# First attention input of a decoder trunk: 32-token blocks of x turned on VectorE, features in the order 512h+4p+k

## The chip, the cores and the metric

The kernel runs on one core of a Trainium2 chip. The metric is the device time of one execution in microseconds; three executions of the kernel before gave a median of 1459.0 us (1458.99 to 1459.35). The input is one sequence of 512 tokens with 1024 features in float32.

TensorE (PE) multiplies; its weight loads are told apart as PEld. VectorE (DVE) and ScalarE (ACT) work on tiles elementwise, GpSimd (POOL) builds small tables and issues some transfers, and SyncE (SP) issues most loads. Each engine executes its instructions in the order in which the program gives them, and semaphores hold an instruction until what it needs is there.

## The reference, cut to what matters

```python
def rms_norm(x, g):
    y = x * lax.rsqrt(jnp.mean(x * x, axis=-1, keepdims=True) + RMS_EPS)
    return y * g

for layer in range(2):
    h = rms_norm(x, norm_mix_pre[layer])
    if layer % 2 == 0:
        h = dilated_attention_mixer(h, attn_w_qkv[j], attn_w_o[j], rel_bias)   # begins with h @ w_qkv
    else:
        h = rglru_mixer(h, ...)                                               # begins with h @ w_in
    x = x + rms_norm(h, norm_mix_post[layer])
    h = rms_norm(x, norm_ffn_pre[layer])
    h = conv_ffn(h, ...)
    x = x + rms_norm(h, norm_ffn_post[layer])
```

The change concerns the very first product, `rms_norm(x, norm_mix_pre[0]) @ w_qkv`. The product sums over the 1024 features, so any order of the features gives the same result as long as x, the norm weights and the rows of `w_qkv` use the same one.

## The kernel before, in words

**Numbers in two parts.** Every float32 operand of a large product is split into a rounded part `hi` (made by ACT) and the rest `lo` (made by DVE), and each product of 128 features is three matmuls: hi x hi, lo x hi, hi x lo.

**Features on the partitions.** TensorE sums over partitions, so x must stand with features on the 128 partitions: `hT` is a pair (hi, lo) of tiles with eight groups of 128 features by 512 tokens. The input x arrives with tokens on the partitions. It is loaded as eight half tiles (`x_half(t, i)`: 128 tokens t, 512 features i), and `first_transposed(t, i)` (L338) turns a half tile by four TensorE transposes of 128 by 128 into one PSUM bank; ACT writes hi from it (L345) and DVE writes lo (L346).

**The norm.** The norm weights multiply the rows of the first weights when those are split (`split_normed`, L139; `whi` on ACT in L143, `wlo` on DVE in L144). The factor of each token, one over the root of its mean square, is applied to the results instead of to x. `first_squares(i)` (L348) sums the squares of four half tiles on ACT, and `first_roots` (L355) makes the factors `first_y`. POOL writes them to memory as a row (`yrow`, L367) and loads the row onto all partitions (`roots`, L368), because queries and keys stand with tokens along the free axis.

**The order of the work.** The order on each engine is the order in which the program is written. Weights come in chunks of 1 MB through three buffers `raw`; `pump` splits them a piece ahead of use into eight pairs of buffers, and `load` issues the next chunk on SP's queue once a buffer is free. The attention begins with `first_values` (L654): the values of the first heads, four token tiles by four weight pieces, each `product(t, u)` six matmuls (L664) of 128 by 512. Between the products stand the eight `first_transposed`, the squares, and the splitting of the weights; the four results are scaled by `first_y` in the end (L707). Then `feat_tiles` makes queries and keys for two heads as four units of 24 matmuls (L255), and `qk` (L649, L651) multiplies each by the `roots` row on DVE. One unit later `local` issues the scores S (L773) of the first head, which need its query and its key.

**The start of the loads.** At the end of the kernel function the first loads are written out by hand: the norm weights as eight rows of 128 (turned by TensorE at L1077 and copied at L1079), then half tiles of x and pieces of the first two weight chunks (`w_part`) in turns, all on SP's queue. A few matmuls on ones (`warm`) come ahead.

Of the kernel before, what the change touches and what calls it, by code (L numbers as in the profile page):

```python
# [18 lines left out]
P = 128  # L19
# [55 lines left out]
def kernel(  # L75
# [42 lines left out]
    def gen(dt=F32, s="g"):  # L118
        return gp.tile([P, 512], dt, tag="g", name=nm(s))

    def psum(s="ps"):
        return pp.tile([P, 512], F32, tag="ps", name=nm(s))
# [86 lines left out]
    def take(i, j):  # L209
        while (i, j) not in units:  # L210
            before = state["live"]
            pump(1)
            assert before != state["live"]
        return units[i, j]

    def done(n=1):
        state["live"] -= n
# [17 lines left out]
            tick()  # L235

    def w_cols(w, c0, normed=False):
        plan.append(("feat", KD, 256, [(w[:, c0 : c0 + 256].rearrange("(k p) c -> p k c", p=P), KD)], 0 if normed else None))

    def w_value(w, *cuts):  # L240

        for i in range(2):
            rows = w[i * 512 : (i + 1) * 512, :]
            plan.append(
                ("value", 4, 512, [(rows[:, c0 : c0 + n].rearrange("(k p) c -> p k c", p=P), n) for c0, n in cuts], 4 * i)
            )

    def w_rows(w, r0):
# [89 lines left out]
    def first_transposed(t, i):  # L338

        ps = psum("tr")  # L340
        for k in range(4 * i, 4 * i + 4):
            nc.tensor.transpose(ps[:, k % 4 * P : (k % 4 + 1) * P], x_sb[:, t, k * P : (k + 1) * P], ident)
        ps3 = ps.rearrange("p (k c) -> p k c", k=4)
        hi, lo = (h[:, 4 * i : 4 * i + 4, t * P : (t + 1) * P] for h in first_hT)
        nc.scalar.activation(hi, ps3, AF.Copy)  # L345
        nc.vector.tensor_tensor(lo, ps3, hi.bitcast(F32), op=ALU.subtract)  # L346

    def first_squares(i):  # L348
        for t in range(4):
            junk = gen(s="junk")  # L350
            nc.scalar.activation(
                junk, x_sb[:, t, i * 512 : i * 512 + 512], AF.Square, accum_out=first_ss[i][:, t : t + 1]
            )
# [249 lines left out]
    def attention(hT, post, pre):  # L603
# [50 lines left out]
        def first_values(vs):  # L654

            ids = [chunk(), chunk()]
            banks = [psum("v") for _ in range(4)]

            def product(t, u, which=range(6)):
                W = take(ids[u // 2], u % 2)  # L660
                steps = [(k, a, b) for a, b in PASSES for k in (2 * u, 2 * u + 1)]
                for n in which:
                    k, a, b = steps[n]
                    mm(  # L664
                        banks[t],
                        hT[a][:, k, t * P : (t + 1) * P],
                        W[b][:, k % 2, :],
                        start=u == n == 0,
                        stop=u == 3 and n == 5,
                    )  # L670

            first_transposed(0, 0)
            warm(WARM - 2)
            product(0, 0, range(4))
            first_transposed(1, 0)
            product(0, 0, range(4, 6))
            product(1, 0)
            product(0, 1, range(3))
            first_transposed(2, 0)
            product(0, 1, range(3, 6))  # L680
            product(1, 1)
            first_transposed(3, 0)
            product(2, 0)
            first_squares(0)
            product(2, 1)
            first_transposed(0, 1)
            product(3, 0)
            take(ids[1], 0)
            first_transposed(1, 1)
            product(3, 1)  # L690
            done(2)
            first_transposed(2, 1)
            product(0, 2)
            take(ids[1], 1)
            first_transposed(3, 1)
            for t in (1, 2, 3):
                product(t, 2)
            first_squares(1)
            y = first_roots()
            first_y.append(y)  # L700
            for t in range(4):
                product(t, 3)
                pump(1)
            done(2)
            for t in range(4):
                o = gen(s="v")
                nc.scalar.activation(o, banks[t], AF.Copy, scale=y[:, t : t + 1])  # L707
                vs.append(o)
# [341 lines left out]
    def w_part(i, k0, k1):  # L1050
        nc.sync.dma_start(raws[i][:, k0:k1, :], plan[i][3][0][0][:, k0:k1, :])

    st = gen(s="st")
    nc.scalar.dma_start(st[:KD, :P], norm_mix_pre[0].rearrange("(k p) -> k p", p=P))
    for i in range(2):
        raws[i] = wp.tile([P, 4, 512], F32, tag="raw", name=nm("raw"), bufs=RAW_BUFS)
    state["dma"] = 2
# [2 lines left out]
    w_part(0, 1, 2)  # L1060
    x_half(1, 0)
    w_part(0, 2, 4)
    x_half(2, 0)
    x_half(3, 0)
    w_part(1, 0, 2)
    x_half(0, 1)
    x_half(1, 1)
    w_part(1, 2, 4)
    x_half(2, 1)
    x_half(3, 1)  # L1070
    one.append(gen(F32R, "one"))
    nc.vector.memset(one[0].bitcast(F32), 1.0)
    warm_ps = psum("warm")
    warm(WARM)
    root_table()
    cols_ps = psum("cols")
    nc.tensor.transpose(cols_ps[:, :KD], st[:KD, :P], ident[:KD, :KD])  # L1077
    first_w.append(cp.tile([P, KD], F32, tag="first_w", name="first_w"))
    nc.vector.tensor_copy(first_w[0], cols_ps[:, :KD])  # L1079
    hT = attention(hT, (norm_mix_post, 0), (norm_ffn_pre, 0))  # L1080
    hT = ffn(0, hT, (norm_ffn_post, 0), (norm_mix_pre, 1))
    hT = lru(hT, (norm_mix_post, 1), (norm_ffn_pre, 1))
# [29 lines left out]
```

## Time and profile before

| | |
|---|---|
| median of three runs | 1459.0 us |
| profiled execution | 1459.46 us |
| its span (first to last instruction) | 1457.7 us |
| PE busy | 1448.4 us (99%) |
| VectorE busy | 862.4 us (59%) |
| ScalarE busy | 669.5 us (46%) |
| GpSimd busy | 134.4 us (9%) |
| moved by DMA | 172.24 MB, 118 GB/s in the mean |

The profile is of one execution. A row of the timeline gives the start in us from the start of the span, the length in us, the engine, the line, the instruction and its operands as out<-in; in square brackets stand the idle time of the engine just before it and who ended that. SPq is SP's queue of issued loads. A row of the groups gives the line, engine, operation and shape with its count, then busy us in total, the mean ns of one, and the idle time before them. The chain of waits follows the work that ended last back through what released it.

### The profile page before, as it was taken

The page shows a single profiled execution, that of the slowest core. Times are in us where ns is not written, and L with a number is a line of the kernel's source. Part 1 is how long each engine was busy: PE and PEld are TensorE (multiplying, and loading weights), DVE is VectorE, ACT ScalarE, POOL GpSimd, SP SyncE. Part 2 cuts the span into 40 slices and gives each one's busy share as a digit, 9 for nine tenths or more (in the row PEclk, how much of TensorE's full clock was granted, in tenths as well). Part 3 has the DMA queues.
Part 4 walks back from the last instruction along what each step waited for, and adds up shares of the span by engine and source line. Part 5 has one row for each costly group of instructions (what it writes and reads, how often), then busy time and mean ns, then how long its engine had stood idle before and what let it go on. Part 6 is the DMA issues. An engine that isn't in the chain of part 4 may idle for free.

```text
span 1457.7 us, 18749 instructions
## 1 busy us (share of the span) xinstructions
PE 1448.4 (99%) x6894; PEld 1217.2 (84%) x6894; DVE 862.4 (59%) x1916; ACT 669.5 (46%) x1516; POOL 134.4 (9%) x275
## 2 busy tenths in 40 slices
PE   9999999999999999999999999999999999999998
PEld 7888888888888898888888888888898888888886
DVE  5656636464646875555654338769776555564333
ACT  6645526262615553443343235589453433444321
POOL 0450513040402100000000001000100000000000
PEclk9999999999999999999999999999999999999999
DMA  6653536364636342322323222432433223223201
GB/s 205 211 151 98 170 117 194 116 180 135 194 120 210 95 137 88 116 87 87 116 87 116 98 90 87 130 116 73 130 102 116 87 94 109 87 98 131 89 1 58
DMA packets 123572, 172.24 MB, mean 118 GB/s; under 512 B 7960, under 2 KB 100600, under 8 KB 123480
## 3 DMA queue, kind: packets, MB, share of 16 engines
q1 hardware_dynamic: 112744, 144.95, 30.7%
q0 software_dynamic: 10144, 25.04, 6.2%
q8 instruction: 54, 0.88, 0.3%
q10 hardware_dynamic: 592, 1.05, 0.2%
q14 instruction: 38, 0.31, 0.1%
HBM read 155.72 MB, written 15.29 MB: 117 GB/s over the span
## 4 chain that ended last, share of the span: by engine, by line
PE 92%; ACT 4%; DVE 3%; issue 1%; DMA 0%; POOL 0%; DVEq 0%; ACTq 0%
PE ps L255 54%; PE acc L255 24%; PE v L723 7%; PE v L664 1%; DVE xb L924 1%; PE S L811 1%; PE O L797 1%; PE O L866 1%; PE S L773 1%; DVE wlo L150 1%; ACT sig L945 1%; ACT whi L149 1%; PE tr L331 1%; DMA ft<-turned 0%; ACT sig L964 0%
## 5 line engine op out<-in xcount | busy, mean ns | idle before, releaser
L255 PE MATMUL ps<-hT,whi 128*128 128x512 f32 (+1 forms) x2752 | 801.4, 375 | 0.0
L255 PEld LDWEIGHTS ps<-hT,whi 128*128 128x128 f32 x2752 | 503.7, 188 | 91.5
L255 PE MATMUL ps<-hT,wlo 128*128 128x512 f32 (+1 forms) x1376 | 515.4, 375 | 0.0
L150 DVE TENSOR_TENSOR wlo<-raw,whi 128x512 fp32r<-128x512 f32 x360 | 230.8, 686 | 187.7 <-ACT whi L149 187.7
L255 PEld LDWEIGHTS ps<-hT,wlo 128*128 128x128 f32 x1376 | 259.1, 188 | 46.5
L149 ACT ACTIVATE whi<-raw 128x512 fp32r<-128x512 f32 x360 | 204.6, 621 | 135.3 <-PE acc L255 120.9
L576 DVE SCALAR_TENSOR_TENSOR u<-ps,cols,u 128x511 f32<-128x511 f32 x192 | 143.8, 749 | 140.2 <-ACT u L572 136.8
L255 PE MATMUL acc<-whi,ahi 128*128 128x512 f32 x512 | 199.7, 390 | 0.0
L255 PE MATMUL acc<-whi,alo 128*128 128x512 f32 x512 | 199.4, 389 | 0.1
L255 PE MATMUL acc<-wlo,ahi 128*128 128x512 f32 x512 | 199.3, 389 | 0.0
L143 ACT ACTIVATE whi<-raw,first_w 128x128 fp32r<-128x128 f32 (+1 forms) x432 | 145.9, 425 | 57.3 <-PE ps L255 33.5
L572 ACT ACTIVATE u<-ps,cols 128x512 f32<-128x512 f32 x96 | 74.8, 779 | 209.3 <-PE ps L255 209.3
L144 DVE SCALAR_TENSOR_TENSOR wlo<-raw,first_w,whi 128x128 fp32r<-128x128 f32 (+1 forms) x432 | 140.3, 390 | 9.3 <-ACT whi L143 9.3
L255 PEld LDWEIGHTS acc<-whi,alo 128*128 128x128 f32 x512 | 96.1, 188 | 20.4 <-DVE alo L150 0.5
L255 PEld LDWEIGHTS acc<-whi,ahi 128*128 128x128 f32 x512 | 96.2, 188 | 19.8
L255 PEld LDWEIGHTS acc<-wlo,ahi 128*128 128x128 f32 x512 | 96.2, 188 | 19.8
L723 PE MATMUL v<-whi,hT 128*128 128x512 f32 x320 | 102.3, 393 | 0.0
L292 POOL DMA_DIRECT2D turned<-T x36 | 19.6, 547 | 761.0 <-DVE T L288 756.2
L299 POOL DMA_DIRECT2D ft<-turned x144 | 79.0, 556 | 42.8 <-issue 17.2
L723 PEld LDWEIGHTS v<-whi,hT 128*128 128x128 f32 x320 | 60.1, 188 | 12.2
L587 ACT ACTIVATE u<-u 128x512 f32<-128x512 f32 x48 | 30.3, 632 | 81.2 <-DVE u L576 81.2
L723 PE MATMUL v<-wlo,hT 128*128 128x512 f32 x160 | 62.3, 390 | 0.0
(160 smaller groups left out, 974.3 us busy)
## 6 DMA issues: line engine op xcount, KB each, us to landing
raw<-in_ffn_w_up_dram SPq DMA_DIRECT2D x48, 1024.0 KB
raw<-in_attn_w_qkv_dram SPq DMA_DIRECT2D x26, 1024.0 KB
raw<-in_ffn_w_down_dram SPq DMA_DIRECT2D x24, 1024.0 KB
raw<-in_attn_w_qkv_dram SPq DMA_DIRECT2D x19, 512.0 KB
raw<-in_lru_w_in_dram SPq DMA_DIRECT2D x8, 1024.0 KB
turned<-T POOLq DMA_DIRECT2D x28, 256.0 KB, 2.7
ft<-turned POOLq DMA_DIRECT2D x112, 64.0 KB, 5.6
vrows<-v SPq DMA_DIRECT2D x16, 256.0 KB
```

The costliest lines, as they stand in the source:

```text
L143: nc.scalar.activation(hi[:, k], raw[:, k], AF.Copy, scale=w)
L144: nc.vector.scalar_tensor_tensor(lo[:, k], raw[:, k], w, hi[:, k].bitcast(F32), op0=ALU.mult, op1=ALU.subtract)
L149: nc.scalar.activation(hi, raw, AF.Copy)
L150: nc.vector.tensor_tensor(lo, raw, hi.bitcast(F32), op=ALU.subtract)
L255: mm(dst, l[a], r[b], start=start and n == 0, stop=stop and n == 2)
L292: nc.gpsimd.dma_start(d, T)
L299: nc.gpsimd.dma_start(t[32 * c : 32 * c + 32].rearrange("j (b x) -> j b x", b=4), d.rearrange("(b j) (c x) -> c j b x", j=32, c=4)[c],)
L331: nc.tensor.transpose(ps[:, k * P : (k + 1) * P], xs[i][:, k * P : (k + 1) * P], ident)
L572: nc.scalar.activation(u, ps, AF.Identity, scale=cc[:, j : j + 1], bias=cc[:, 48 + j : 49 + j])
L576: nc.vector.scalar_tensor_tensor(u[:, d:], ps[:, : S - d], wc, u[:, d:], op0=ALU.mult, op1=ALU.add)
L587: nc.scalar.activation(u, u, AF.Gelu_apprx_tanh)
L723: mm(banks[t], hT[a][:, k, t * P : (t + 1) * P], W[b][:, k % 2, :], start=(k, a, b) == (0, 0, 0), stop=(k, a, b) == (KD - 1, 1, 0),)
```

## The change

The features get the order 512h+4p+k: in each half h of 512 features, partition p holds the four neighbouring features 4p to 4p+3, one in each group k. The rows of the normed weights are read to match, so a chunk `feat` comes as two loads of 512 rows instead of one load of 1024, and the norm weights are loaded straight into that shape.

Two half tiles, (0,0) and (1,0), are still turned by TensorE, which now reads every fourth feature. The other six are loaded a second way by `x_part`: four loads of 64 KB, each of which puts 32 tokens of each of four blocks, with 128 features, on 32 partitions. In that shape a transpose of 32 by 32 blocks on VectorE, `first_turned`, brings the features onto the right partitions; ACT and DVE then make hi and lo from this tile instead of from PSUM. The token-major halves of these six, which the sums of squares and later the residual need, are loaded after all parts, four of them only after the first loads of the next weights. In `first_values` the six transposes are replaced by `first_turned` at other places between the products, `first_squares(0)` moves behind the third weight piece and `first_squares(1)` with `first_roots` into the loop over the fourth.

```diff
     def w_cols(w, c0, normed=False):
-        plan.append(("feat", KD, 256, [(w[:, c0 : c0 + 256].rearrange("(k p) c -> p k c", p=P), KD)], 0 if normed else None))
+        if normed:
+            srcs = [(w[i * 512 : (i + 1) * 512, c0 : c0 + 256].rearrange("(p k) c -> p k c", k=4), 4) for i in range(2)]
+        else:
+            srcs = [(w[:, c0 : c0 + 256].rearrange("(k p) c -> p k c", p=P), KD)]
+        plan.append(("feat", KD, 256, srcs, 0 if normed else None))
...
-                ("value", 4, 512, [(rows[:, c0 : c0 + n].rearrange("(k p) c -> p k c", p=P), n) for c0, n in cuts], 4 * i)
+                ("value", 4, 512, [(rows[:, c0 : c0 + n].rearrange("(p k) c -> p k c", k=4), n) for c0, n in cuts], 4 * i)
...
         ps = psum("tr")
         for k in range(4 * i, 4 * i + 4):
-            nc.tensor.transpose(ps[:, k % 4 * P : (k % 4 + 1) * P], x_sb[:, t, k * P : (k + 1) * P], ident)
-        ps3 = ps.rearrange("p (k c) -> p k c", k=4)
+            nc.tensor.transpose(
+                ps[:, k % 4 * P : (k % 4 + 1) * P],
+                x_sb[:, t, i * 512 : i * 512 + 512].rearrange("t (p k) -> t k p", k=4)[:, k % 4], ident,
+            )
+        first_split(t, i, ps)
+
+    def first_split(t, i, src):
+        src = src.rearrange("p (k c) -> p k c", k=4)
         hi, lo = (h[:, 4 * i : 4 * i + 4, t * P : (t + 1) * P] for h in first_hT)
-        nc.scalar.activation(hi, ps3, AF.Copy)
-        nc.vector.tensor_tensor(lo, ps3, hi.bitcast(F32), op=ALU.subtract)
+        nc.scalar.activation(hi, src, AF.Copy)
+        nc.vector.tensor_tensor(lo, src, hi.bitcast(F32), op=ALU.subtract)
+
+    def first_turned(t, i):
+
+        T = gen(s="T")
+        nc.vector.transpose(
+            T.rearrange("p (k b c) -> p b k c", k=4, b=4), x_blocks[t, i].rearrange("p (b j k) -> p b k j", b=4, k=4)
+        )
+        first_split(t, i, T)
...
             first_transposed(1, 0)
             product(0, 0, range(4, 6))
             product(1, 0)
-            product(0, 1, range(3))
-            first_transposed(2, 0)
-            product(0, 1, range(3, 6))
+            product(0, 1)
+            first_turned(2, 0)
+            for t in range(4):
+                x_half(t, 1)
             product(1, 1)
-            first_transposed(3, 0)
+            first_turned(3, 0)
             product(2, 0)
-            first_squares(0)
             product(2, 1)
-            first_transposed(0, 1)
+            first_turned(0, 1)
+            take(ids[1], 0)
             product(3, 0)
-            take(ids[1], 0)
-            first_transposed(1, 1)
+            first_turned(1, 1)
             product(3, 1)
             done(2)
-            first_transposed(2, 1)
             product(0, 2)
+            first_turned(2, 1)
             take(ids[1], 1)
-            first_transposed(3, 1)
-            for t in (1, 2, 3):
+            product(1, 2)
+            first_turned(3, 1)
+            for t in (2, 3):
                 product(t, 2)
-            first_squares(1)
-            y = first_roots()
-            first_y.append(y)
+            first_squares(0)
             for t in range(4):
                 product(t, 3)
                 pump(1)
+                if t == 0:
+                    first_squares(1)
+                    y = first_roots()
+                    first_y.append(y)
             done(2)
...
-    st = gen(s="st")
-    nc.scalar.dma_start(st[:KD, :P], norm_mix_pre[0].rearrange("(k p) -> k p", p=P))
+    first_w.append(cp.tile([P, KD], F32, tag="first_w", name="first_w"))
+    nc.scalar.dma_start(
+        first_w[0].rearrange("p (i k) -> p i k", i=2), norm_mix_pre[0].rearrange("(i p k) -> p i k", i=2, k=4)
+    )
+    x_blocks = {}
+
+    def x_part(t, i):
+
+        x_blocks[t, i] = o = gen(s="xb")
+        src = x[0, t * P : (t + 1) * P, i * 512 : (i + 1) * 512].rearrange("(b j) f -> j b f", j=32)
+        for a in range(4):
+            nc.sync.dma_start(o[32 * a : 32 * a + 32].rearrange("j (b f) -> j b f", b=4), src[:, :, a * P : (a + 1) * P])
...
     x_half(1, 0)
     w_part(0, 2, 4)
+    x_part(2, 0)
+    x_part(3, 0)
+    w_part(1, 0, 2)
+    x_part(0, 1)
+    x_part(1, 1)
+    w_part(1, 2, 4)
+    x_part(2, 1)
+    x_part(3, 1)
     x_half(2, 0)
     x_half(3, 0)
-    w_part(1, 0, 2)
-    x_half(0, 1)
-    x_half(1, 1)
-    w_part(1, 2, 4)
-    x_half(2, 1)
-    x_half(3, 1)
...
-    cols_ps = psum("cols")
-    nc.tensor.transpose(cols_ps[:, :KD], st[:KD, :P], ident[:KD, :KD])
-    first_w.append(cp.tile([P, KD], F32, tag="first_w", name="first_w"))
-    nc.vector.tensor_copy(first_w[0], cols_ps[:, :KD])
```

## The prediction

> **What bounds the kernel now.** I read the page first, then the chain of waits over the first 80 us (the change touches nothing later except how weight rows are ordered), then the timeline of each engine there.
>
> ```profile
> span 1457.7 us, 18749 instructions
> PE 1448.4 (99%) x6894; PEld 1217.2 (84%) x6894; DVE 862.4 (59%) x1916; ACT 669.5 (46%) x1516; POOL 134.4 (9%) x275
> PE 92%; ACT 4%; DVE 3%; issue 1%; DMA 0%; POOL 0%; DVEq 0%; ACTq 0%
> ```
>
> TensorE is busy for 99% of the span. So work taken off PE shortens the run one for one, and any new wait of PE lengthens it one for one; nothing later gives it back. The chain view of the first stage (start, length, what) shows the pieces at stake:
>
> ```profile
> 14.46 0.44 PE tr L342 x4
> ...
> 19.47 0.44 PE tr L342 x4
> 19.91 1.39 PE v L664 x6
> 21.30 0.44 PE tr L342 x4
> ...
> 23.57 9.55 PE v L664 x42
> 33.12 27.20 PE ps L255 x120
> 60.31 1.52 PE S L773 x8
> ```
>
> The transposes L342 stand on the path with no wait around them. 42 matmuls in 9.55 us are 0.227 us each, so one product of six is 1.364 us. From 19.47 to 21.30, 1.83 us, stand one transposed half tile and one product: a half tile costs 1.83 - 1.364 = 0.47 us of PE. The 120 matmuls from 33.12 are five weight units of 24 (5.44 us each) for query and key; behind them stand the score matmuls S, which need the first head's query and key.
>
> **The change, part by part.** All positions are in the profiled execution; it took 1459.46 us (span plus 1.76), 0.46 above the median of 1459.0, and I add the same difference to the median. A measurement of this kernel can tell 0.2%, 2.9 us, from no change.
>
> *Removed from PE.* Six half tiles: 6 x 0.47 = 2.8 us. The transpose of the norm weights goes too, and the next one moves from 4.10 to its place, 0.2 us earlier:
>
> ```profile
> 3.90 0.27 PE L1077 MATMUL cols<-ident,st 8*128 8x8 f32 x1
> 4.10 1.11 PE L342 MATMUL tr<-ident,x_sb 128*128 128x128 f32 x4
> 5.75 1.33 ACT L143 ACTIVATE whi<-raw,first_w 128x512 fp32r<-128x512 f32 x2
> ```
>
> Together 3.0 us, if PE stayed the bound. The norm weights now come straight by their own load; they are first used at 5.75, and the load that feeds the transposed form is done before 3.90.
>
> *Added to VectorE.* Each of the six now takes a 32x32 transpose on DVE (T), the rounding copy on ACT (hi), and the subtraction on DVE (lo). DVE executes in order and lo stands directly behind its T in the built program, so while ACT makes hi, DVE stands still. Durations:
>
> ```profile
> 10.18 1.41 DVE L144 SCALAR_TENSOR_TENSOR wlo<-raw,first_w,whi 128x512 fp32r<-128x512 f32 x2
> 21.77 0.60 ACT L345 ACTIVATE hT<-tr 128x512 fp32r<-128x512 f32 x1 [1.23 <-PE tr L342]
> 22.40 0.69 DVE L346 TENSOR_TENSOR hT<-tr,hT 128x512 fp32r<-128x512 f32 x1 [1.03 <-ACT hT L345]
> L288 DVE STREAM_TRANSPOSE T<-L 128x512 f32<-128x512 f32 x22 | 14.8, 694 | 3.3 <-ACT L L786 2.9 <-DMA ft<-turned 0.4
> L372 DVE COPY roots<-roots x1: 612/612/612, 161.2 to 161.2; 128x512 f32<-128x512 f32 x1
> 32.95 0.62 PE L255 MATMUL ps<-hT,whi 128*128 128x512 f32 x2
> ```
>
> One turned half tile holds DVE for 0.69 + 0.60 + 0.69 = 1.98, with the hand-overs (0.03 between ACT's end at 22.37 and lo at 22.40) about 2.0 us; the product it feeds takes PE 1.364. DVE therefore becomes the bound of this stage. Its last old work is the weight split that starts at 10.18 and ends at 11.59; 0.2 earlier is 11.4. Then come six turned half tiles (12.0) and two weight pairs (2 x 1.36): 26.1. The last hi is ready 0.7 before that, at 25.4. Behind it PE has products (3,2) and (0..3,3) left, 5 x 1.364 = 6.8, so the first L255 matmul starts at 32.2 instead of 32.95. Of the 3.0 us PE spends 2.2 waiting, and 0.75 is left.
>
> The new T reads every fourth float, which no transpose of before does. Copy L372 reads SBUF with the same step and needs 0.612 for 512 elements, less than L288, so I take no price; twice L288's duration would add 6 x 0.69 = 4.1. SBUF — State Buffer of the Trainium skill (section Door 1: The DMA port swizzle, its note on cachelines) says that each access to a new 16-byte line pays a penalty, which speaks against a step of four floats; it gives no figure, and L372, with that step, agrees with no penalty on DVE. The two half tiles that PE still transposes load eight blocks with that step:
>
> ```profile
> L342 PEld LDWEIGHTS tr<-ident,x_sb x32: 137/141/230, 4.1 to 23.2; 128*128 128x128 f32 x32
> ```
>
> Free or twice 0.141 for four loads in each of two tiles, 0 to 1.1; part overlaps matmuls; a wider step cannot be quicker. I take 0.2, nearest to free.
>
> *Moved: the sums of squares.* They need the token-major x, now loaded last, and stand on ACT behind the last hi; the second four stand also behind the first weight unit for q.
>
> ```profile
> 24.10 0.62 ACT L351 ACTIVATE junk<-x_sb 128x512 f32<-128x512 f32 x1
> 25.94 0.61 ACT L351 ACTIVATE junk<-x_sb 128x512 f32<-128x512 f32 x1
> 27.19 9.47 ACT L143 ACTIVATE whi<-raw,first_w 128x128 fp32r<-128x128 f32 x32
> 27.93 0.16 DVE L365 SCALAR_TENSOR_TENSOR first_y<-s,first_y 128x4 f32<-128x4 f32 x1
> 28.39 0.89 POOL L367 DMA_DIRECT2D yrow<-first_y  x1 [27.08 <-DVE wlo L144]
> 38.37 0.56 POOL L368 DMA_DIRECT2D roots<-yrow  x1 [9.08 <-DMA yrow<-first_y]
> 45.30 0.69 DVE L649 SCALAR_TENSOR_TENSOR qk<-ps,roots 128x512 f32<-128x512 f32 x1 [8.26 <-DMA roots<-yrow]
> 45.91 4.29 DVE L144 SCALAR_TENSOR_TENSOR wlo<-raw,first_w,whi 128x128 fp32r<-128x128 f32 x16
> 54.92 0.68 DVE L651 TENSOR_TENSOR qk<-ps,roots 128x512 f32<-128x512 f32 x1
> ```
>
> Squares stand 0.61 apart; the roots are done at 28.09, 2.15 after the last one starts. After: four squares 25.3 to 27.75; eight rounding copies at 9.47/32 = 0.296, to 30.1; the last square starts at 30.1 + 3 x 0.61 = 31.95; roots at 34.1, 6.0 later than before. Everything behind shifts along: the two transfers by POOL (28.39 to 45.2), the first use of the roots (45.30), and behind it on DVE, which runs in order without a gap, 16 splits, the second query, 16 splits, and the first key, done at 55.60. With 6.0 that is 61.6, with 0.2 for the wider loads 61.8. S starts at 60.31 before, so it has 4.7 us of slack over its key; now PE gets there at 60.31 - 0.55 = 59.76 and waits 2.1 us. S starts about 61.85, 1.5 us late. PE's four units before it are covered: their splits precede the wait, and the fifth is wanted at 54 and split from 52. POOL's bias rows stand behind the roots too; the scores that read them stand on DVE behind the same wait, so they meet as before.
>
> *Loads.* SP issues 24 parts of 64 KB, then the six token-major halves (1.5 MB again), then the q and k weights as two halves each. In the built program each SP load waits until the one eight before it has landed.
>
> ```profile
> 3.09 0.94 SPq L1048 DMA_DIRECT2D x_sb<-in_x_dram  x2
> 9.03 0.33 SPq L1048 DMA_DIRECT2D x_sb<-in_x_dram  x1
> 6.00:12.00 6.00, 5.21 (x23) 3.42 (x23) 3.93 (x6) 2.89 (x5) 0.00 (x0) 1.00 0.98 348
> turned<-T POOLq DMA_DIRECT2D x28, 256.0 KB, 2.7
> ```
>
> Issues stand 0.47 apart. The load that waits for the third piece of the first weights goes at 9.03 before; after, this is the eighth part, and five loads ahead of it are the same, so it goes at 9.03 again. Behind it stand 31 issues: a weight piece, eight parts, a weight piece, eight parts, two halves of x, three bias rows, four halves of q and k weights, four halves of x. The last part is issued at 9.5 + 17 x 0.47 = 17.5 and lands near 20; its T wants it at 24.0. The first q half is issued at 9.5 + 23 x 0.47 = 20.3; from it on 3.1 MB at 348 GB/s take 9.0, and 2.2 for start and landing (under the 2.7 row) bring the last token-major half to 31.5. Its square wants it at 31.95: hidden by 0.4 us. Without that cover each 0.1 us on the issue step costs 2.3 us.
>
> *Nothing for the rest.* The new row order leaves each contiguous piece of a weight row at 256 or 512 columns. The 24 second issues sit on SP, which stands waiting for buffers that DVE frees (53.2 us in eight waits in the first 80), and at 0.47 each they vanish in that; without it they would cost 0.47 us per load.
>
> ```profile
> SPq L199 <- DVE wlo L144: 53.2, 8, 12.7
> ```
>
> **Sum.** -0.2 (norm weights) - 2.8 (transposes) + 2.25 (PE waits for DVE) + 0.2 (wider loads) + 2.05 (S waits for its key) = +1.5: 1459.0 + 1.5 = 1460.5.
>
> **The rivals.**
>
> *Slower: the loads pace the roots.* The deciding point is an issue step above 0.56 us, where the last token-major half lands at 33.5 and the end is 2.9 us late. The nearest row for the small shape is POOL's, also 32 partitions by four pieces:
>
> ```profile
> DMA to landing us min/median/max: 3.9/5.4/6.9
> ```
>
> Eight in flight at 5.4 us give a step of 0.68: first q half at 9.5 + 23 x 0.68 = 25.1, last half at 25.1 + 11.2 = 36.3, roots 4.3 later still, end +5.8: 1464.8. For it: 64 KB per landing. Against it: those went through POOL, and 348 GB/s was reached with eight loads in flight.
>
> *Slower still: PE's clock falls in that wait.* In the loads' case PE idles over 4 us ahead of S. The granted clock reads 1.00 in the stage quoted above, and the longest gap of PE before is the 1.47 at its start; the first five matmuls behind that tell a price:
>
> ```profile
> 1.47 2.50 PE L1040 MATMUL warm<-one 128*128 128x512 f32 x5 [1.47 <-DVE one L1072]
> ```
>
> 0.50 each instead of 0.227; if five run so again, 1.4 us more: 1466.2. TensorE: Matmul & The Clock Gate (Part 1) in the Trainium skill has the clock halve after an idle window of about 3.4 us; no run here shows it, and in my forecast the wait is 2.1 us.
>
> *Hidden.* If the two transfers of the roots take 2 us or more less than 16.8, S waits for nothing and 0.55 is won: 1458.4. Against it: they are two small transfers as before.
>
> *Faster: DVE keeps up.* If ACT's step overlapped another T, PE would win 2.8 and, with early halves, S's wait would go: 1456.2. The order T, lo, T, lo in the built program speaks against it.
>
> **How the numbers follow.** Forecast (+0.3 to +2.9): 0.52. Loads pace the roots: 0.24. With the clock: 0.08. Hidden (-0.8 to +0.3): 0.12. Faster: 0.04. The range runs from the lower end of the hidden case, 1458.2, to the loads' case, 1464.8; it leaves out the faster case, the clock and some tail, under 0.2. Faster by over 0.2%: 0.04; within: 0.52 + 0.12 = 0.64; slower: 0.32.
>
> **What would show it.** In the profile after: DVE's waits for hi of about 0.6 us before each of six lo; PE waiting before product (3,2) by about 2 us; first L255 matmul near 32.2; the roots done near 34.3; the first key near 61.8 and PE idle before S by about 2 us; x halves landing before ACT asks for them. A T above 0.75 us, ACT waiting on x_sb, or S starting without a wait would prove a step wrong.

## The result, and the profile after

The changed kernel takes 1466.6 us (median of six, 1464.2 to 1467.9) against 1459.0 (1458.99 to 1459.35): 7.6 us longer, a ratio of 1.005 with the interval 1.004 to 1.006. The forecast was 1460.5 with a range to 1464.8, so the time lies 6 us above the forecast and 1.8 above the range, in the direction that was named. The profiled execution took 1466.16 us, 6.7 more than that of before, and all comparisons of positions below are between these two.

The page shows the saving on TensorE and that it was not kept:

```profile
span 1464.3 us, 18788 instructions
PE 1448.3 (99%) x6869; PEld 1215.0 (83%) x6869; DVE 868.2 (59%) x1921; ACT 670.0 (46%) x1516; POOL 133.6 (9%) x275
```

25 instructions fewer on PE, but the busy time is the same (1448.4 before) and the span is 6.6 us longer: something made PE wait, and something made its remaining work longer. The chain of waits (start, length, what) shows where. First the kernel before, the two lines behind those that the prediction shows, then the kernel after:

```profile
61.83 5.49 PE ps L255 x24
67.32 1.52 PE S L773 x8
```

```profile
25.60 8.70 DMA x_sb<-in_x_dram
34.32 1.35 ACT junk L369 x4
...
39.82 13.44 DMA raw<-in_attn_w_qkv_dram
...
64.88 0.61 DVE qk L669
...
65.53 2.04 PE S L794 x8
67.57 6.84 PE ps L259 x24
74.40 1.52 PE S L794 x8
```

Before, the chain over this stretch is PE alone. After, it runs through loads, the squares on ACT, loads again, DVE's key, and only then PE. The first S starts 5.2 us later (65.53 against 60.31), and by the second S the delay has grown to 7.1 (74.40 against 67.32): the 24 matmuls between them take 6.84 instead of 5.49, and the eight of S 2.04 instead of 1.52.

The timeline of TensorE has all its marked waits between 10 us and the second S in four rows. With them stand a pair of matmuls that took longer than its neighbours (19.45) and the start of the query and key units (34.59):

```profile
19.45 0.91 PE L682 MATMUL v<-wlo,hT 128*128 128x512 f32 x2
...
21.55 0.72 PE L682 MATMUL v<-whi,hT 128*128 128x512 f32 x2 [0.71 <-ACT hT L355]
23.95 0.73 PE L682 MATMUL v<-whi,hT 128*128 128x512 f32 x2 [0.75 <-ACT hT L355]
27.66 0.73 PE L682 MATMUL v<-whi,hT 128*128 128x512 f32 x2 [2.05 <-ACT hT L355]
34.59 0.62 PE L259 MATMUL ps<-hT,whi 128*128 128x512 f32 x2
65.53 2.04 PE L794 MATMUL S<-qk,qk 128*128 128x128 f32 x8 [3.58 <-DVE qk L669]
```

The first three waits add up to 3.5 us in the first stage, more than the 3.0 us that PE was spared, but the units start 1.64 us later (34.59 instead of 32.95), and 3.5 less 3.0 is only 0.5. The starts of the rows give the rest. From 21.55 to 23.95 pass 2.40 us for one product (1.364) and a wait of 0.75, so each wait cost some 0.29 us more than its idle time, and the pair at 19.45 took 0.91 where other pairs take 0.62. Together PE lost about 4.7 us there (an estimate from these rows). The last row is the wait for the first key. Who is late there is read off DVE and ACT:

```profile
L361 DVE STREAM_TRANSPOSE T<-xb x6: 1068/1082/1095, 11.2 to 25.9; 128x512 f32<-128x512 f32 x6
...
13.01 0.69 DVE L356 TENSOR_TENSOR hT<-T,hT 128x512 fp32r<-128x512 f32 x1 [0.70 <-ACT hT L355]
...
36.94 0.16 DVE L383 SCALAR_TENSOR_TENSOR first_y<-s,first_y 128x4 f32<-128x4 f32 x1
55.18 0.69 DVE L667 SCALAR_TENSOR_TENSOR qk<-ps,roots 128x512 f32<-128x512 f32 x1 [11.47 <-DMA roots<-yrow]
64.80 0.68 DVE L669 TENSOR_TENSOR qk<-ps,roots 128x512 f32<-128x512 f32 x1
```

```profile
27.51 0.61 ACT L369 ACTIVATE junk<-x_sb 128x512 f32<-128x512 f32 x1
...
34.32 0.63 ACT L369 ACTIVATE junk<-x_sb 128x512 f32<-128x512 f32 x1 [0.70 <-DMA x_sb<-in_x_dram]
```

A transpose with the step of four floats takes 1.08 us (the three numbers are shortest, median, longest in ns). DVE stands 0.70 us for ACT before each low split. The squares begin at 27.51, ACT waits 0.70 us for a half tile of x that lands at 34.3, the roots are done at 37.10 instead of 28.09, and their row is first used 18.1 us later. The windows around S (us, then busy of PE, PEld, DVE, ACT, POOL with counts, granted PE clock, DMA share, GB/s) show why PE is slower behind the wait:

```profile
58.00:61.50 3.50, 3.50 (x17) 2.92 (x16) 3.50 (x13) 1.37 (x3) 0.00 (x0) 1.00 0.34 73
61.50:65.50 4.00, 0.45 (x2) 0.03 (x1) 4.00 (x15) 0.16 (x1) 0.00 (x0) 1.00 0.76 260
65.50:67.00 1.50, 1.47 (x8) 1.34 (x9) 1.50 (x3) 1.48 (x3) 0.00 (x0) 0.98 0.36 101
67.00:68.00 1.00, 1.00 (x4) 0.82 (x3) 1.00 (x2) 0.97 (x1) 0.00 (x0) 0.50 1.06 373
68.00:69.00 1.00, 1.00 (x3) 0.79 (x3) 1.00 (x3) 0.00 (x0) 0.00 (x0) 0.50 1.06 358
69.00:70.00 1.00, 1.00 (x4) 0.74 (x3) 1.00 (x3) 0.00 (x0) 0.00 (x0) 0.50 0.76 233
70.00:71.00 1.00, 1.00 (x5) 0.82 (x4) 1.00 (x5) 0.00 (x0) 0.00 (x0) 0.83 1.03 346
```

The granted clock is 1.00 through the wait and falls to 0.50 about 1.5 us after work has resumed, for a little over 3 us. So the 7.1 us by which the second S is late divide, from these rows, into 1.6 in the first stage, 3.6 of waiting for the first key, and 1.9 of slower matmuls (0.52 in S and 1.35 in the 24 behind it). Of the 7.1 the span keeps 6.6: at 260.87 the kernel before waits 0.25 us for a tile that a DMA brings, the changed kernel comes there later and does not wait, and behind that place it is 6.6 us late.

### The profile page after: what moved, and what is told of

Same layout as the page of the kernel before. It is cut to its first block, busy times and chain, and to the rows that moved or that the text cites. A ratio compares the mean times of both kernels' runs of the same rounds, so it can differ in the third digit from the quotient of the medians.

```text
span 1464.3 us, 18788 instructions
## 1 busy us (share of the span) xinstructions
PE 1448.3 (99%) x6869; PEld 1215.0 (83%) x6869; DVE 868.2 (59%) x1921; ACT 670.0 (46%) x1516; POOL 133.6 (9%) x275
## 4 chain that ended last, share of the span: by engine, by line
PE 88%; ACT 4%; DVE 4%; DMA 3%; issue 1%; SPq 0%; DVEq 0%; ACTq 0%
PE ps L259 53%; PE acc L259 24%; PE v L744 7%; DMA raw<-in_attn_w_qkv_dram 2%; DVE xb L945 1%; PE O L887 1%; PE S L832 1%; DMA x_sb<-in_x_dram 1%; PE O L818 1%; PE S L794 1%; DVE wlo L150 1%; DVE wlo L144 1%; ACT sig L966 1%; ACT whi L149 1%; PE tr L335 1%
## 5 line engine op out<-in xcount | busy, mean ns | idle before, releaser
L259 PEld LDWEIGHTS acc<-wlo,ahi 128*128 128x128 f32 x512 | 96.1, 188 | 19.9
```

What stands on the lines that cost most here:

```text
L259: mm(dst, l[a], r[b], start=start and n == 0, stop=stop and n == 2)
```

## The experiments

My theory after the result: the first S waits for a key, the key for the roots, and the roots come late for two reasons, VectorE's chain of turned tiles and the loads; the wait then costs the clock as well. The rivals were a first stage limited by something else, the loads alone, and the feature order itself. The medians of the kernel before, beside which these ran, were 1459.0, 1459.8 and 1459.5 us in the three groups; ratios are to those.

**1. The step of the transpose (t_contig).**

```diff
-  x_blocks[t, i].rearrange("p (b j k) -> p b k j", b=4, k=4)
+  x_blocks[t, i].rearrange("p (b k j) -> p b k j", b=4, k=4)
```

> The changed kernel, but each of the six T reads its half tile in runs of 32 neighbouring floats instead of every fourth float, so that the six half tiles come out in another feature order than the weights have. Theory (the step of four floats in the read costs the 1.08 us): T falls from 1.08 to 0.69 us, the first query matmul comes 6 x 0.39 = 2.3 us earlier, at about 32.3. The roots stay within 0.8 us of 37.1, since the token-major halves of x land at 34.3, so S still starts near 65 us and the time falls by under 1 us, to about 1466. Rival (T is long for another reason: freshly landed parts, the write side, or loads into the same memory): T stays at 1.08. Second rival (the DVE chain alone sets the roots): the time falls by 2.3, to 1464.3.

The turned features then meet other rows of the weights, so this run is for its time alone. Measured: 1466.6 us, ratio 1.0049 (1.0034 to 1.0064), as the changed kernel.

```profile
L361 DVE STREAM_TRANSPOSE T<-xb x6: 703/705/707, 11.3 to 24.0; 128x512 f32<-128x512 f32 x6
...
33.14 0.63 ACT L369 ACTIVATE junk<-x_sb 128x512 f32<-128x512 f32 x1 [2.95 <-DMA x_sb<-in_x_dram]
...
57.03 0.50 PE L259 MATMUL ps<-hT,wlo 128*128 128x512 f32 x1 [2.28 <-DVE wlo L144]
66.37 1.79 PE L794 MATMUL S<-qk,qk 128*128 128x128 f32 x8 [2.44 <-DVE qk L669]
```

The step costs 0.38 us of 1.08, and without it the first unit starts at 32.38 instead of 34.59, as forecast. No time comes of it: ACT now waits 2.95 us for the half tiles of x, the roots are as late as ever, and PE waits 2.28 us for the fifth unit's low splits, which stand on DVE behind the wait for the roots, and 2.44 for the key. The windows behind the first of these waits (columns as above) show that it too cost clock:

```profile
58.00:59.00 1.00, 1.00 (x4) 0.79 (x4) 1.00 (x6) 1.00 (x3) 0.38 (x1) 0.62 0.42 71
...
60.00:61.00 1.00, 1.00 (x4) 0.78 (x3) 1.00 (x5) 0.14 (x1) 0.00 (x0) 0.50 0.25 74
61.00:62.00 1.00, 1.00 (x5) 0.79 (x4) 1.00 (x4) 0.00 (x0) 0.00 (x0) 0.67 0.00 0
```

Had the price of the transpose in the prediction been right, the kernel would still have been slow.

**2. The clock in the wait (keep_warm).**

```diff
+            if h == 0:
+                keep = psum("keep")
+                for _ in range(14):
+                    mm(keep, first_hT[0][:, 0, :P], first_hT[0][:, 0, :], start=True, stop=True)
             for a in range(4):          # the matmuls of S
```

> The changed kernel with 14 matmuls of 128x512 on the first features, result unused, on PE directly ahead of the first head's scores S. 14 x 0.227 = 3.2 us lie inside the 3.6 us for which PE waits there. Theory (the wait lets PE's granted clock fall to 0.50 for about 3 us behind S): the granted clock stays at 1.00 through 60 to 80 us, the 24 matmuls behind S take 5.4 instead of 6.8 us, S starts where it did, and the time falls by 1.7 us, to about 1464.9. Rival (the slow matmuls behind S come from the loads that run at the same time or from the waiting itself): no change, 1466.6.

Measured: 1465.5 us, ratio 1.0043 (1.0028 to 1.0058). The chain behind the wait:

```profile
66.24 1.79 PE S L798 x8
68.02 5.47 PE ps L259 x24
```

S is no earlier (66.24 against 65.53), but the clock reads 1.00 in every window to 74 and the 24 matmuls take 5.47 us again, beside the same loads. In the medians this is worth 1.1 us, less than the 1.7 expected. The fall of the clock is a consequence of the wait and the smaller part of its price.

**3 and 4. S one feature group later, in the changed kernel (s_later) and in the kernel before (before_s_later).**

```diff
-  side(local(2 * hp + hh, hh, q, k, v), 1 + hh)
+  side(local(2 * hp + hh, hh, q, k, v), (2 if hp == 0 else 1) + hh)
```

> The changed kernel with the local attention of the first two heads begun one unit of 24 matmuls later, so S stands 5.44 us of PE work further back. Theory (of the 6.6 to 7.6 us lost, 1.6 are lost in the first stage on VectorE's chain, 3.6 in PE's wait ahead of S and 1.7 in the low clock behind it): PE waits under 0.3 us ahead of S, the clock stays at 1.00, the time is 1459.0 + 1.6 = 1460.7, at most 1461.5. Rival (the late roots starve PE anyway, through weight splits that stand behind them on VectorE or through PSUM banks): a wait of 2 us or more shows up at another place and the time stays above 1463.

> The kernel before, with the same move of the first two heads' local attention by one unit. A control: S waits for nothing in the kernel before (slack 4.7 us), so the move itself should cost nothing: 1459.0, within 0.3 us. If it gains or loses more, that amount has to be taken off the result of the same move in the changed kernel.

Measured: 1461.8 us, ratio 1.0017 (1.0007 to 1.0027), and for the control 1459.5, ratio 1.0002 (0.9993 to 1.0011). The first is 0.3 above the most that was expected. In the changed kernel S then stands at 68.29 with no wait, and 4.8 of the 7.6 us are gone. Between the two 2.3 us are left, in the medians and at S (68.29 against 65.99). The first stage is 1.7 of them (the units start at 35.02 against 33.35). The rest arises in the fifth unit, where the low splits stand on DVE behind the late roots and PE waits for one:

```profile
57.70 0.50 PE L259 MATMUL ps<-hT,wlo 128*128 128x512 f32 x1 [0.31 <-DVE wlo L144]
```

**5. The feature order alone, in the kernel before (order_alone).** Only these parts of the change, with the value weights in the same order and the norm weights loaded straight into their tile (not shown):

```diff
-  srcs = [(w[:, c0 : c0 + 256].rearrange("(k p) c -> p k c", p=P), KD)]
+  srcs = [(w[i * 512 : (i + 1) * 512, c0 : c0 + 256].rearrange("(p k) c -> p k c", k=4), 4) for i in range(2)]
...
-  nc.tensor.transpose(ps[...], x_sb[:, t, k * P : (k + 1) * P], ident)
+  nc.tensor.transpose(ps[...], x_sb[:, t, i * 512 : i * 512 + 512].rearrange("t (p k) -> t k p", k=4)[:, k % 4], ident)
```

> The kernel before, with nothing but the new feature order: the weights of the normed products loaded as four neighbouring rows to a partition, the norm weights loaded by one DMA straight into their tile, TensorE's transposes reading x with a step of four floats; no turned tiles, loads and order of the work as before. If the feature order itself is free, as the prediction had it: 1459.0 (1458.6 to 1459.6), first product matmul behind the split of the last tile near 32.8, first S matmuls at 60.1 to 60.4. If the strided reads of TensorE or the new shape of the weight loads carry part of the loss: 1460.5 or more, with weight units or transposes that take longer than before.

Measured: 1460.3 us, ratio 1.0004 (0.9995 to 1.0013), so no difference that these runs can tell, though the median lies above the range that I gave. The reading with a step shows in the weight loads of the transposes:

```profile
L346 PEld LDWEIGHTS tr<-ident,x_sb x32: 195/209/226, 3.8 to 23.1; 128*128 128x128 f32 x32
```

They take 209 ns instead of 141, and the first unit starts at 32.91 (32.95 before). The roots are done as early as before, but their first use comes at 47.52 instead of 45.30, so in this execution 2.2 us of the slack of S went; whether the order of the features or its two loads per chunk did that, one profile does not show.

**6. The second halves of x loaded earlier (x_early).**

```diff
     x_half(2, 0)
     x_half(3, 0)
+    for t in range(4):
+        x_half(t, 1)
...
             first_turned(2, 0)
-            for t in range(4):
-                x_half(t, 1)
```

> The changed kernel with the four second halves of x (token-major) issued in the starting list, right behind the halves of tiles 2 and 3, instead of from inside the first product. They land near 27 instead of 34.3, the bias rows and q/k weights some 2 us later. Theory (VectorE's turned tiles and the late squares behind them set the roots; the loads cost only the 0.70 of wait that ScalarE shows): roots done 36.3 to 36.5 instead of 37.1, first S at 64.7, 1465.5 (1464.5 to 1466.2). Rival (the loads set the roots): roots done at or below 34.5, wait at S under 1.5, no fall of the clock, 1462 to 1463.

Measured: 1468.1 us, ratio 1.0057 (1.0043 to 1.0070), outside both ranges. ACT's wait for x is gone and the roots are done at 36.34, as the theory had it. But nothing of that reaches the key. The write of the roots, issued 0.76 us earlier than in the changed kernel (36.65 against 37.41), ends at the same time, and the row is first used 1.0 us later:

```profile
47.64 0.56 POOL L386 DMA_DIRECT2D roots<-yrow  x1 [10.10 <-DMA yrow<-first_y]
...
56.22 0.69 DVE L667 SCALAR_TENSOR_TENSOR qk<-ps,roots 128x512 f32<-128x512 f32 x1 [13.27 <-DMA roots<-yrow]
...
66.56 3.36 PE L792 MATMUL S<-qk,qk 128*128 128x128 f32 x8 [4.05 <-DVE qk L669]
```

The roots' time of being done is therefore not the whole story. From the issue of the row's load to its first use pass 8.6 us here, 7.5 in the changed kernel and up to 8.4 in other runs with that kernel's loads, so why the last 1.0 us were lost stays open. PE's wait grows to 4.05 us, and the clock reads 0.50 from 65 to 71, twice as long as in the changed kernel; both make the run slower still.

**7 and 8. The turned tiles in a pipeline, early halves, squares in one go (pipe_early), and the same with S one group later (pipe_early_s).** These are three edits at once; the early halves are those of experiment 6. `first_turned` now only makes and returns T, and the split comes one tile later:

```diff
-            first_turned(2, 0)
-            product(1, 1)
-            first_turned(3, 0)
+            T = first_turned(2, 0)
...
+            Tn = first_turned(3, 0)
+            first_split(2, 0, T)
+            product(1, 1)
+            T = first_turned(0, 1)
+            first_split(3, 0, Tn)
...
             first_squares(0)
+            first_squares(1)
+            y = first_roots()
             for t in range(4):
                 product(t, 3)
```

> The changed kernel with three edits of order: each VectorE transpose is issued one tile ahead of the low split before it, so that a tile asks VectorE for 1.08 + 0.69 = 1.77 us and not for 2.46; the four second halves of x are issued in the starting list; all squares and the roots come ahead of the last quarter of the first product, as in the kernel before. Theory (the serial chain transpose, high split, low split costs the first stage, the late roots the rest): first product matmul behind the last split at 30 to 31 instead of 34.6, roots done 31 to 33, first S at 58 to 60 with a wait of at most 1.5, granted clock 1.00, 1457.5 (1456.3 to 1459.0), so the transposes that TensorE no longer does show as time. Rival (VectorE's time for the six transposes is the limit, in whatever order): first product matmul not under 33, 1461 or more.

> The kernel of the run before this one, with the first head's S matmuls one feature group later, as in the run that moved them alone. Theory: the rest of the wait ahead of S goes, S between 61 and 64 with no wait, and what TensorE no longer does in the first stage is all of the difference: 1456.4 (1455.6 to 1457.8). Rival (the wait at S is already gone in the kernel of the run before this one, and the move only puts work late): equal to it or up to 0.5 slower.

Measured: 1463.6 us, ratio 1.0023 (1.0012 to 1.0033), and with S later 1458.0, ratio 0.9987 (0.9978 to 0.9996); both lie above the expected ranges. In pipe_early PE waits nowhere between 13 and 54 us, the first unit starts at 30.97, the roots are done at 30.51, all as the theory wanted. Of the three edits the pipeline must be what freed the first stage: the early halves alone left the first unit at 34.64 (experiment 6), and the squares stand on ACT behind the last turned tile. Yet:

```profile
30.81 0.89 POOL L385 DMA_DIRECT2D yrow<-first_y  x1 [29.49 <-DVE first_y L383]
45.85 0.56 POOL L386 DMA_DIRECT2D roots<-yrow  x1 [14.15 <-DMA yrow<-first_y]
...
53.23 0.69 DVE L667 SCALAR_TENSOR_TENSOR qk<-ps,roots 128x512 f32<-128x512 f32 x1 [12.96 <-DMA roots<-yrow]
...
63.58 3.36 PE L797 MATMUL S<-qk,qk 128*128 128x128 f32 x8 [4.05 <-DVE qk L669]
```

The write of the roots to memory, 512 single floats, keeps POOL waiting 14.15 us instead of 9.08. The loads run at 310 to 350 GB/s from 28 to 36 us here, and have ended by 30 in the kernel before; in both the write ends about 9 us after the loads. My expectation for S (58 to 60) missed this: PE waits 4.05 us for the key, and the clock falls while it still waits and stays down for over 6 us:

```profile
60.00:62.00 2.00, 0.00 (x0) 0.00 (x0) 2.00 (x9) 0.00 (x0) 0.00 (x0) 0.90 1.00 376
62.00:63.00 1.00, 0.00 (x0) 0.00 (x0) 1.00 (x5) 0.00 (x0) 0.00 (x0) 0.50 0.56 213
...
68.00:69.00 1.00, 1.00 (x5) 0.80 (x4) 1.00 (x5) 0.00 (x0) 0.00 (x0) 0.79 0.93 316
```

Where S stands later, a part of the gain of the first stage shows.

**9 and 10. A shorter trip of the roots, in the changed kernel (after_rows) and in pipe_early (pipe_early_rows).**

```diff
-  nc.gpsimd.dma_start(row.rearrange("t p -> p t"), y)
+  yT = cp.tile([P, 32], F32, tag="yT", name="yT")
+  nc.vector.transpose(yT, y32)          # y is the first four columns of the zeroed y32
+  for b in range(4):
+      nc.gpsimd.dma_start(row[:, 32 * b : 32 * b + 32], yT[32 * b : 32 * b + 4, :])
```

> The changed kernel with a shorter trip of the roots to DRAM and back: VectorE turns the 128x4 roots (in a zeroed 128x32 tile) and POOL writes them as four DMAs of four rows of 128 bytes, 16 packets where the kernel has 512 of 4 bytes that take 10 us to land. Roots done 37.1 as before. Theory (the first S waits for a key that waits for the roots row): first use of the roots at 48 to 51 instead of 55.2, first S at 62 to 63 with no wait, no fall of the clock, 1461.7 (1460.8 to 1462.8), as in the run that moved S. Rival (the keys are held by the weight splits of their own unit on VectorE, and the roots only seem to be the last): first S not before 65, 1465 or more.

> The kernel with the three edits of order (transposes one tile ahead, early second halves of x, squares and roots ahead of the last quarter), with that same shorter trip of the roots; S where the changed kernel has it. There the roots are done at 30.5, but their 512 small packets were issued into a load stream that runs to 37 and landed at 45.7. Theory: row landed by 38, first use of the roots at 43 to 46 instead of 53.2, no wait at S, first product matmul behind the last split at 31, 1456.8 (1456.0 to 1458.2). Rival (the loads of x that is read twice hold the 256 KB row as they held the 4-byte packets): first use at 49 or later, a wait of 1 us or more at S, 1459 or more.

The 512 and 16 named there are the pieces that the program writes; the profile counts 32 packets for the one DMA and 128 for the four. Measured: 1462.1 us, ratio 1.0016 (1.0007 to 1.0025), and 1457.8, ratio 0.9990 (0.9981 to 0.9999). In after_rows:

```profile
40.97 0.58 POOL L390 DMA_DIRECT2D roots<-yrow  x1 [1.60 <-DMA yrow<-yT]
...
45.31 0.69 DVE L671 SCALAR_TENSOR_TENSOR qk<-ps,roots 128x512 f32<-128x512 f32 x1 [2.09 <-DMA roots<-yrow]
...
61.84 1.68 PE L798 MATMUL S<-qk,qk 128*128 128x128 f32 x8
```

Roots done at 36.6 reach their first use at 45.31, not 55.18, and S waits for nothing: the same gain as from moving S, by another hand. That the late roots hold S is thereby shown twice.

The shorter write frees more than the roots. Weights for the next units are issued from 39 us on in both kernels, and the chain of the changed kernel runs through them (39.82, 13.44 us). The windows of the changed kernel and of after_rows, in this order, show that they hardly moved beside the write of single floats:

```profile
36.00:48.00 12.00, 12.00 (x55) 9.93 (x54) 7.34 (x29) 11.90 (x38) 1.19 (x2) 1.00 0.27 28
36.00:48.00 12.00, 12.00 (x54) 9.95 (x53) 9.77 (x38) 12.00 (x39) 8.74 (x32) 1.00 0.60 195
```

They carry 28 GB/s against 195; keep_warm and s_later, which also write single floats, carry 26 and 38 from 42 to 48 us. So the rows shorten two waits at once, for the roots and for the weights, and this experiment does not part them; in the changed kernel DVE waited for the roots last, at 55.18. In pipe_early_rows the first use comes at 44.10 and S at 59.78, without a wait. This version and pipe_early_s are the two that beat both kernels, by 1.7 and 1.9 us in the medians of their groups; both intervals end just below 1, so the gain is small and barely clear of the noise. Of the 3.0 us that PE no longer spends on transposes, that is what these versions keep.

**11. The loads alone, in the kernel before (before_double).** The 24 block loads of the change are added behind the loads of x; nobody reads them.

```diff
     x_half(3, 1)
+    for t, i in ((2, 0), (3, 0), (0, 1), (1, 1), (2, 1), (3, 1)):
+        o = gen(s="xb")
+        ...                            # four loads of 32 partitions each, as in x_part
```

> The kernel before, with 24 loads of 64 KB more, that nobody reads: the six half tiles of x that the change loads by blocks, in the same pieces on the same queue, behind the eight halves of x and ahead of the bias rows and the q/k weights. Everything else as before. Theory (what the loads cost by themselves is covered there: the roots have 4.7 us to spare before the first S): bias rows and q/k weights issued 8 to 11 us later, first use of the roots later by 2 to 6 us, first S still between 60 and 61.5, 1459.5 (1459.0 to 1460.8). Rival (reading x twice on one queue is the price of the change): first S at 63 or later, 1462 or more.

Measured: 1459.6 us, ratio 0.9999 (0.9990 to 1.0008). The first use of the roots moves from 45.30 to 48.26, and S stands at 60.19 without a wait. Loading x a second time, in blocks, costs no time by itself while the roots have their slack; in this execution it takes 3 us of it.

**12. No step, and S later (t_contig_s).** The edits of 1 and 3 together; as in 1, the turned features meet other rows of the weights.

> The changed kernel with both single edits tried before: VectorE's transpose reads its input without the step of four floats (features then meet other rows of the weights: that part of the result is changed), and the first head's S matmuls stand one feature group later. Alone, the first moved the first product matmul from 34.6 to 32.4 and no time, since S waited for its key all the same. Theory: with S out of the way the 2.2 us show: 1459.6 (1458.8 to 1460.4), which is what the prediction's 0.69 us for the transpose would have given. Rival (the first stage has another limit than VectorE's six transposes): 1461.0 or more.

Measured: 1461.1 us, ratio 1.0013 (1.0005 to 1.0022), 1.5 above the expectation and hardly below s_later. By its number this went to the rival. The profile names two things beside the transposes:

```profile
8.97 0.75 PE L346 MATMUL tr<-ident,x_sb 128*128 128x128 f32 x4 [0.90 <-DMA x_sb<-in_x_dram]
...
57.10 0.50 PE L259 MATMUL ps<-hT,wlo 128*128 128x512 f32 x1 [1.27 <-DVE wlo L144]
```

In that execution the second half tile of x landed about 1 us late, and the first unit started at 33.46 (32.38 in the same kernel with S in its old place); and the fifth unit's splits, behind the late roots on DVE, made PE wait 1.27 us. So an earlier first stage runs into the roots again, at the unit before S. How much of the remaining 1.5 us is the one and how much the other, one profile cannot say.

## Why the prediction was wrong

**The transpose's price: wrong, and the first step that failed.** T was taken at 0.69 us, with no penalty for the step of four floats, because copy L372 reads with the same step in 0.612. It took 1.08; without the step 0.70. Six times 0.38 is 2.3 us; the first unit was forecast for 32.2 and came at 34.59. The term "PE waits for DVE" was 2.25; the waits measured 3.5, and about 4.7 with what PE lost at their edges. The prediction's upper bound, twice L288's duration, held the true price; the row that decided, the copy L372, was the wrong kind of instruction. The note on lines of 16 bytes in SBUF — State Buffer (Door 1: The DMA port swizzle) of the Trainium skill spoke against the choice, and experiment 1 agrees with it for this instruction.

**The serial order T, hi, lo: right.** DVE waits 0.70 us before each of the six low splits, as said. Experiment 7 shows it as a cost: with T one tile ahead the same durations leave no wait on PE from 13 us to the end of the stage.

**The squares and roots: right in mechanism, short in size.** Done at 37.1 against a forecast of 34.3. The first square starts 2.2 us later than forecast (27.51 against 25.3), from the transposes, and 0.7 is ACT's wait for x.

**The loads: "hidden by 0.4 us" was wrong.** The issue step was nearly as forecast (eight parts in 3.86 and in 4.33 us, 0.48 to 0.54), the first half of the q weights was issued at 20.85 (20.3), but the last halves of x landed from 34.3 on instead of at 31.5. The sum let 3.1 MB move at 348 GB/s from the issue of that half on. From 18 to 24 us the queue moved only 182 GB/s in the mean, and 292 from 24 to 26; from 26 on it moved about 360. The windows between the issue at 20.85 and the landing at 34.3 add up to some 4.1 MB (an estimate). So two things failed: the rate did not hold at the start, and some 1 MB more moved in that time than was counted. Whether that was still in flight at 20.85 or belongs to weights issued behind the halves is not shown. Experiment 1 shows this as a second cause in its own right: with a cheap transpose the loads alone keep the roots at 37.5. The rival "the loads pace the roots" was thus partly what happened, but not by a slower issue step, on which it was priced.

**The roots' trip: 17.2 us from done to first use before, taken to shift along unchanged; 18.1 measured.** It is no constant: the runs with the changed kernel's loads lie between 18.1 and 19.1, and experiments 7 and 8, where loads still run when the roots are written, took 22.7. The 19.9 of experiment 6 is not far enough outside to name a cause.

**The wait at S: right in mechanism, 3.6 us instead of 2.1.** The key was forecast for 61.8 and was done at 65.48.

**The clock: put down as a rival that the forecast's shorter wait excludes; it happened.** The prediction priced five slow matmuls at 1.4 us; 24 matmuls and S took 1.9 us more than before, and keeping PE busy won 1.1. The rule of TensorE: Matmul & The Clock Gate (Part 1) in the Trainium skill, a halved clock after some 3.4 us without work, agrees with 3.58 us and 0.50 here, but experiment 1 has the same fall behind a wait of 2.28 us and none behind one of 2.44, and in experiments 6 and 7 the clock fell 2.5 and 2.1 us after PE had stopped, while it still waited. The measurements decide: a wait of 2.1 us, as forecast, is no safe distance from this fall.

**Nothing for the rest: right in time.** Experiment 5 finds no cost of the feature order that its runs can tell, though in its profile 2.2 us of the slack of S are gone. "Nothing later gives it back" was wrong by 0.5 us, the wait at 260.87.

**The sum, by its terms.** The first stage was put at -0.55 (-0.2 - 2.8 + 2.25 + 0.2) and came at +1.64; the wait at S was put at +2.05 and came at +3.58; the clock was put at nothing and took 1.9; 0.5 came back later. Together +1.5 became +6.6 in the spans of the profiled executions.

## What to carry to other kernels

Work moved from a busy engine to an idle one pays only if the idle one keeps its distance: here a serial transpose, rounding and subtraction per tile made VectorE the bound of the first stage until the transpose was issued one tile ahead. Before moving a side result such as the roots, follow its whole trip to the first use, memory and back included, and compare it with its slack; a slack of 4.7 us covered the second loading of x alone (experiment 11), not the sum. Take the price of an operation with an unusual step from the same instruction, or carry both bounds in the forecast.

## What the runs showed of the hardware that was not expected

A 128x512 float32 transpose on VectorE takes 1.08 us when it reads every fourth float and 0.70 when it reads in a row, while a copy with that step takes 0.61 for as many elements; TensorE's weight loads with that step take 209 ns instead of 141. The granted clock fell to 0.50 behind or within waits of PE of 2.28, 3.58 and 4.05 us and not after one of 2.44; it stayed there for a little over 3 us in the first two and over 6 in the third, so the length of the wait alone does not decide. Writing 128x4 floats to memory as 512 single floats kept POOL waiting 9 to 10 us where the loads in front of it had ended, and 14 us beside running loads; the loads issued behind it moved at 28 GB/s in the mean (36 to 48 us), against 195 with the shorter write. Turned first and written as 16 rows of 128 bytes, from the end of the transpose to the issue of the row's load it took 4.1 us (36.84 to 40.97). The number of packets does not explain it: the profile counts 32 for the first write and 128 for the second.
